# First score block and last weighing block over 128 columns instead of 256 in a hybrid encoder block on Trainium2

## The chip, the cores and the metric

The kernel runs on one core of one Trainium2 chip. The core has a matrix engine (TensorE, PE in the profile, with PEld for its weight loads), VectorE (DVE), ScalarE (ACT), GpSimd (POOL) and SyncE (SP, which issues the large loads). The metric is the time of one execution on the device in microseconds (us); several runs are given by their median.

## The reference

One layer over 512 positions and 1024 features, in float32. The part that matters here is the attention: 16 heads of 64 features over chunks of 64 positions, in which each position reads its own chunk and the 8 chunks before it. With 512 positions that is everything up to the end of its own chunk.

```python
def reference(x, ...):
    xn = rmsnorm(h, norm_mix_g[l])
    u = jnp.einsum('bsd,de->bse', xn, w_in[l])
    q, k, v, xr, gr, ga, gb = jnp.split(u, splits, axis=-1)
    ya = chunked_band_attention(q, k, v, rel_table[l]) @ w_attn_out[l]
    ...                                   # conv and RG-LRU branch: hr
    yb = (hr * jax.nn.gelu(gr)) @ w_rnn_out[l]
    ...                                   # g_a, g_b: gates
    h = h + (g_a * ya + g_b * yb) @ w_o[l]
    hn = rmsnorm(h, norm_ffn_g[l])
    g, up = jnp.split(hn @ w_ffn_in[l], 2, axis=-1)
    h = h + (jax.nn.silu(g) * up) @ w_ffn_out[l]
    return rmsnorm(h, final_norm_g)

def chunked_band_attention(q, k, v, rel_table):
    ...
    s = jnp.einsum('bnqhd,bnkhd->bhnqk', q, kb) * scale + bias     # own chunk and 8 before
    s = jnp.where(valid[None, None, :, None, :], s, NEG_INF)
    p = jax.nn.softmax(s, axis=-1)
    o = jnp.einsum('bhnqk,bnkhd->bnqhd', p, vb)
```

## The kernel before

**Precision.** A float32 operand is split into two parts of a reduced type, fp32r: hi is the rounded value, lo the rest (`split`, L78 to L81: a copy on ScalarE at L80, a subtraction on VectorE at L81). A projection (`mm3`, L72 to L76) is three matmuls: hi with hi, hi with lo, lo with hi. In the profile's rows these operands are printed as f32. Every matmul is preceded by its own weight load.

**Order of the work.** First come a norm, the recurrent branch and the gates, then the attention of 16 heads, then the output projections and a feed-forward part. A scheduler orders the instructions of each engine when the program is built; the source order is only its input. The attention's loop over heads calls `transposed`, `scores` of the next head, `weigh`, and between them `fill`, which puts in projections of q, k, v and a gate that are ready, so that TensorE has work while the softmax runs. These projections use 512 moving columns (v: 256).

**Scores** (`scores`, L611). The 512 queries are 4 blocks of 128 (`qb`). Block `qb` sees the keys of blocks 0 to `qb`, w = (qb + 1) x 128 columns. Two matmuls (L624 with the hi part of k, L625 with the lo part) write w columns into PSUM, for `qb` = 0 however 256, of which 128 are used. VectorE adds the bias and takes the row's maximum (L627), ScalarE takes the exponential and the sum (L628), VectorE the reciprocal (L629), GpSimd scales (L631).

**Transposes** (`transposed`, L634). The probabilities are transposed by TensorE in 10 pieces of 128 x 128 (L643) into three PSUM tiles: keys of block 0 (512 columns of queries), block 1 (384), and blocks 2 and 3 together (256 + 128). They are split into `pp` (L645, through L80 and L81). In the third tile `pp[2]` the columns 256 to 384 are filled with zeros by GpSimd (L637), and the columns of key block 3 are put behind them, at 384 to 512, by a split of their own.

**Weighing** (`weigh`, L652). For each key block, two matmuls (hi and lo of `pp`, L663) add values times probabilities into the last n query columns of one PSUM tile: n is 512, 384, 256 and, for the last key block, 256 again, where the first 128 of these columns are the zeros.

Of the kernel before, what the change touches and what calls it, by code (L numbers as in the profile page):

```python
# [36 lines left out]
def block_kernel(ctx: ExitStack, tc: tile.TileContext, x, norm_mix_g, w_in, b_merge, rel_table,  # L37
# [3 lines left out]
    pe, dve, act, pool, sp = nc.tensor, nc.vector, nc.scalar, nc.gpsimd, nc.sync  # L41
# [4 lines left out]
    def opened(name, bufs=1, side="left"):  # L46
        st = ExitStack()
        return st, st.enter_context(pool_of(name, bufs, side))
# [17 lines left out]
    def f(ap):  # L66
        return ap.bitcast(F32)

    def mm_tile(name, tag="mm"):
        return ps.tile([P, S], F32, tag=tag, bufs=4 if tag == "mm" else 2, name=name)  # L70
# [7 lines left out]
    def split(hi, lo, src):  # L78

        act.activation(hi, src, AF.Copy)  # L80
        dve.tensor_sub(lo, src, f(hi))  # L81
# [311 lines left out]
    def bias_tile(h):  # L393
        b = aw.tile([P, S], F32, tag="bias", bufs=2, name=f"bias{h}")
        src = ext_d[h:h + 1, 0:S]
        band = bass.AP(tensor=src.tensor, offset=src.offset, ap=[[1, P], [1, S]])
        sp.dma_start(out=b[:], in_=band)
        pool.memset(b[64:128, 448:512], NEG)
        return b
# [150 lines left out]
    def blocks(ap):  # L550
        return ap.rearrange("p (b i) -> p b i", i=P)

    def backwards(ap):
        return blocks(ap)[:, :, ::-1]

    def halves(e):
        own, other = slice(e * HD, e * HD + HD), slice(HD - e * HD, 2 * HD - e * HD)
        return own, other
# [52 lines left out]
    def scores(h):  # L611
        pr, e = divmod(h, 2)
        q, kh, kl = qk[pr]
        bias = bias_tile(h)
        lsum = cp.tile([P, NT], F32, tag="lsum", bufs=2, name=f"l{h}")
        nmax = cp.tile([P, NT], F32, tag="nmax", bufs=2, name=f"m{h}")
        rl = cp.tile([P, NT], F32, tag="rl", bufs=2, name=f"rl{h}")
        prob = [aw2.tile([P, (qb + 1) * P], F32, tag=f"p{qb}", name=f"p{h}_{qb}") for qb in range(NT)]
        for qb in range(NT):
            w = (qb + 1) * P  # L620
            wm = max(w, 256)
            sc = mm_tile(f"s{h}_{qb}") if qb == 2 else ps.tile([P, S], F32, tag="s", bufs=2, name=f"s{h}_{qb}")
            qs = q[:, e, qb * P:(qb + 1) * P]
            pe.matmul(sc[:, 0:wm], qs, kh[:, e, 0:wm], start=True, stop=False)  # L624
            pe.matmul(sc[:, 0:wm], qs, kl[:, e, 0:wm], start=False, stop=True)  # L625

            dve.tensor_tensor_reduce(prob[qb][:], sc[:, 0:w], bias[:, S - w:S], -1.0, 3e38, ALU.add, ALU.min, nmax[:, qb:qb + 1])  # L627
            act.activation(prob[qb][:], prob[qb][:], AF.Exp, bias=nmax[:, qb:qb + 1], scale=-1.0, accum_out=lsum[:, qb:qb + 1])  # L628
        dve.reciprocal(rl[:], lsum[:])  # L629
        for qb in range(NT):  # L630
            pool.tensor_scalar(prob[qb][:], prob[qb][:], rl[:, qb:qb + 1], 1.0, ALU.mult, ALU.mult)  # L631
        return prob

    def transposed(h, prob):  # L634

        pp = [aw2.tile([P, 2, S], F32R, tag="pt", bufs=4, name=f"pp{h}_{i}") for i in range(3)]
        pool.memset(f(pp[2][:, :, 256:384]), 0.0)  # L637
        for i, kbs in enumerate(((0,), (1,), (2, 3))):
            pt = ps.tile([P, S], F32, tag="t", bufs=2, name=f"pT{h}_{i}")
            for kb in kbs:  # L640
                for qb in range(kb, NT):
                    at = qb - min(kb, 2) if kb < 3 else 2
                    pe.transpose(pt[:, at * P:(at + 1) * P], prob[qb][:, kb * P:(kb + 1) * P], ident[:])  # L643
            for at, lo, n in (((0, 0, 512),), ((0, 0, 384),), ((0, 0, 256), (384, 256, 128)))[i]:
                split(pp[i][:, 0, at:at + n], pp[i][:, 1, at:at + n], pt[:, lo:lo + n])  # L645
        return pp

    aT = []
# [3 lines left out]
    def weigh(h, pp):  # L652
        pr, e = divmod(h, 2)
        own, other = halves(e)
        if e == 0:
            oacc.append(tg_.tile([P, S], F32, tag="tg", name=f"oacc{pr}"))
        acc = oacc[pr]
        po = mm_tile(f"o{h}")
        for kb in range(NT):
            i, lo, n = ((0, 0, 512), (1, 0, 384), (2, 0, 256), (2, 256, 256))[kb]  # L660
            st = vs[pr // 2][kb][:, pr % 2, 2 * e:2 * e + 2].rearrange("p a d -> p (a d)")
            for part in range(2):
                pe.matmul(po[:, S - n:S], st, pp[i][:, part, lo:lo + n], start=kb == 0 and part == 0, stop=kb == NT - 1 and part == 1)  # L663
        act.activation(acc[own, :], po[other, :], AF.Copy)
        dve.tensor_add(acc[own, :], po[own, :], acc[own, :])
        if e == 1:
            if pr % 2 == 0:
                aT_pairs.append(rnp.tile([P, 2, 2, S], F32R, tag="big", bufs=4, name=f"aT{pr}"))
            o = aT_pairs[-1][:, pr % 2]
            split(blocks(o[:, 0]), blocks(o[:, 1]), backwards(acc[:]))  # L670
            aT.append(o)
# [23 lines left out]
    for j in range(KT):  # L695
        if j == 6:
            prob = scores(0)
        po = mm_tile(f"po_yb{j}")
        project(po, weights(f"yb{j - j % 2}"), j % 2, rnn)
        dve.scalar_tensor_tensor(zB[j], zB[j], 1.0, po[:], ALU.add, ALU.mult)  # L700
    for h in range(HEADS):
        pp = transposed(h, prob)
        if h + 1 < HEADS:
            prob = scores(h + 1)
        fill(1.25 + 1.5 * h)
        weigh(h, pp)
        fill(2.0 + 1.5 * h)
# [115 lines left out]
    sc_stack, sc = opened("sc", 2)  # L823
# [100 lines left out]
    for i, ((t, at), po) in enumerate(zip(pieces, pos)):  # L924
        for k0, wf in zip(ks[late:], wfs):
            out_tile(t, po, k0, wf, at)
        n = 1 + i // 4
# [30 lines left out]
```

## Time and profile before

| | |
|---|---|
| median of 3 runs | 896.61 us (894.88 to 899.5) |
| profiled execution, time | 896.52 us |
| profiled execution, span | 894.7 us |
| granted TensorE clock | 0.995 |
| TensorE busy | 876.4 us, 5220 matmuls |
| VectorE, ScalarE, GpSimd busy | 554.3, 474.0, 133.4 us |
| score matmuls | 235 to 431 us after the span's start |
| weighing matmuls | 261 to 454 us |

The profile is of one execution. Busy time of TensorE counts each matmul's record from start to modelled end; neighbouring records overlap. A row of a group names the source line, the engine, the operation, output and inputs, the shape, the count, then busy time and mean length, then the idle time of the engine ahead of the group and what ended it.

### The profile page before, as it was taken

What the parts mean: (1) busy time and instruction counts of PE and PEld (TensorE: products, weight loads), DVE (VectorE), ACT (ScalarE), POOL (GpSimd) and SP (SyncE); (2) the same over time, 40 slices, a digit from 0 to 9 for tenths busy, and PEclk for the clock granted to TensorE, in tenths of its full rate; (3) what the DMA queues carried; (4) which work ended last, traced back from release to release, by engine and by line L of the source; (5) the groups of instructions that cost most, each with busy time, mean ns of one, the idle gap of its engine ahead of it and who ended that gap; (6) DMA issues with size and microseconds to landing.
All of it is one profiled execution on the core that took longest, in us unless ns stands there. A gap on an engine that the chain in (4) does not pass through costs nothing.

```text
span 894.7 us, 13342 instructions
## 1 busy us (share of the span) xinstructions
PE 876.4 (98%) x5220; PEld 779.1 (87%) x5220; DVE 554.3 (62%) x863; ACT 474.0 (53%) x841; POOL 133.4 (15%) x168
## 2 busy tenths in 40 slices
PE   8999999999999999999999999899999999999997
PEld 5988888888888889797888889899999999888886
DVE  6776556563466676566547455998788887463203
ACT  7566546642257666566533365556555556722203
POOL 4012112120013222232100002500000001300200
PEclk9999999999999999999999999999999999999999
DMA  7323223433332232232223521333433333253102
GB/s 263 95 72 117 85 83 93 119 95 95 106 106 72 84 105 61 75 105 68 68 69 126 210 76 43 95 119 98 139 95 95 96 106 107 95 189 121 43 1 95
DMA packets 85023, 89.05 MB, mean 100 GB/s; under 512 B 5344, under 2 KB 73552, under 8 KB 84960
## 3 DMA queue, kind: packets, MB, share of 16 engines
q1 hardware_dynamic: 83584, 84.73, 30.6%
q10 hardware_dynamic: 1376, 3.47, 1.0%
q8 instruction: 41, 0.67, 0.3%
q14 instruction: 22, 0.18, 0.1%
HBM read 86.05 MB, written 2.14 MB: 99 GB/s over the span
## 4 chain that ended last, share of the span: by engine, by line
PE 92%; DVE 3%; ACT 2%; DMA 1%; issue 1%; POOL 1%; SPq 0%; DVEq 0%; POOLq 0%; ACTq 0%
PE po_out L74 5%; PE po_out L76 4%; PE po_out L75 4%; PE p_fu L76 2%; PE p_fu L75 2%; PE p_fu L74 2%; PE p_fg L74 2%; PE p_fg L75 2%; PE p_fg L76 2%; PE o L663 2%; PE pT L643 2%; PE po_ga L74 2%; PE po_q L75 2%; PE po_q L74 2%; PE q_fg L76 2%; PE po_ga L75 2%
## 5 line engine op out<-in xcount | busy, mean ns | idle before, releaser
L75 PE MATMUL po_out<-whl_fo,act_hi 128*128 128x512 f32 (+1 forms) x198 | 72.4, 366 | 0.0
L74 PE MATMUL po_out<-whl_fo,act_hi 128*128 128x512 f32 (+1 forms) x198 | 72.4, 366 | 0.0
L76 PE MATMUL po_out<-whl_fo,act_lo 128*128 128x512 f32 (+1 forms) x198 | 71.6, 365 | 0.0
L81 DVE TENSOR_TENSOR whl_fo<-raw_fo,whl_fo 128x1024 fp32r<-128x1024 f32 x22 | 27.6, 1262 | 45.5 <-ACT whl_fo L80 45.1
L631 POOL TENSOR_SCALAR p<-p,rl 128x128 f32<-128x128 f32 (+1 forms) x64 | 37.6, 611 | 83.2 <-DVE rl L629 82.6
L80 ACT ACTIVATE whl_fo<-raw_fo 128x1024 fp32r<-128x1024 f32 x22 | 22.9, 1056 | 49.3 <-PE po_out L76 33.9
L628 ACT ACTIVATE p<-p,m 128x128 f32<-128x128 f32 (+3 forms) x64 | 35.5, 556 | 20.1 <-DVE m L627 19.8
L627 DVE CUSTOM_DVE_ANT_0 p<-s,bias 128x128 f32<-128x128 f32 (+3 forms) x64 | 29.8, 487 | 22.4 <-PE s L625 21.6
L76 PEld LDWEIGHTS po_out<-whl_fo,act_lo 128*128 128x128 f32 x198 | 37.3, 189 | 6.0
L75 PEld LDWEIGHTS po_out<-whl_fo,act_hi 128*128 128x128 f32 x198 | 37.4, 189 | 6.0
L74 PEld LDWEIGHTS po_out<-whl_fo,act_hi 128*128 128x128 f32 x198 | 37.4, 189 | 5.9
L663 PE MATMUL o<-pp,v 128*128 128x256 f32 (+2 forms) x128 | 35.3, 336 | 3.0 <-ACT pp L80 3.0
L843 POOL TENSOR_TENSOR act_lo<-act,act_hi 128x1024 fp32r<-128x1024 f32 x4 | 10.5, 2622 | 185.6 <-ACT act_hi L842 184.1
L75 PE MATMUL po_v<-whl_v,xnT 128*128 128x256 f32 x128 | 36.9, 288 | 0.0
L81 DVE TENSOR_TENSOR pp<-pT,pp 128x256 fp32r<-128x256 f32 (+2 forms) x64 | 30.4, 486 | 10.4 <-ACT pp L80 9.9
L74 PE MATMUL po_v<-whl_v,xnT 128*128 128x256 f32 x128 | 36.6, 286 | 0.0
L76 PE MATMUL po_v<-whl_v,xnT 128*128 128x256 f32 x128 | 36.4, 285 | 0.0
L80 ACT ACTIVATE pp<-pT 128x256 fp32r<-128x256 f32 (+2 forms) x64 | 26.6, 433 | 10.7 <-DVE pp L81 6.3
L75 PE MATMUL po_xr<-xnT,whl_xr 128*128 128x512 f32 (+1 forms) x80 | 27.9, 354 | 1.0 <-DVE xnT L331 1.0
L81 DVE TENSOR_TENSOR whl_fu_s<-s_fu,whl_fu_s 128x1024 fp32r<-128x1024 f32 x20 | 25.3, 1280 | 5.8 <-ACT whl_fu_s L80 5.7
L643 PE MATMUL pT<-ident,p 128*128 128x128 f32 x160 | 27.5, 273 | 0.8 <-POOL p L631 0.7
L663 PEld LDWEIGHTS o<-pp,v 128*128 128x128 f32 x128 | 22.8, 189 | 5.9 <-ACT pp L80 1.8
(354 smaller groups left out, 3096.0 us busy)
## 6 DMA issues: line engine op xcount, KB each, us to landing
raw_fg<-in_w_ffn_in_dram SPq DMA_DIRECT2D x22, 512.0 KB, 4.5
raw_fu<-in_w_ffn_in_dram SPq DMA_DIRECT2D x22, 512.0 KB, 3.5
raw_fo<-in_w_ffn_out_dram SPq DMA_DIRECT2D x22, 512.0 KB, 4.3
raw_qk<-in_w_in_dram SPq DMA_DIRECT2D x32, 256.0 KB, 3.2
raw_xr<-in_w_in_dram SPq DMA_DIRECT2D x8, 512.0 KB, 4.7
raw_gr<-in_w_in_dram SPq DMA_DIRECT2D x8, 512.0 KB, 3.4
raw_ga<-in_w_in_dram SPq DMA_DIRECT2D x8, 512.0 KB, 3.8
raw_gb<-in_w_in_dram SPq DMA_DIRECT2D x8, 512.0 KB, 3.5
```

The lines of the kernel that those rows point to most:

```text
L74: pe.matmul(o, sh, mh, start=start, stop=False, skip_group_check=parts)
L75: pe.matmul(o, sh, ml, start=False, stop=False, skip_group_check=parts)
L76: pe.matmul(o, sl, mh, start=False, stop=stop, skip_group_check=parts)
L80: act.activation(hi, src, AF.Copy)
L81: dve.tensor_sub(lo, src, f(hi))
L627: dve.tensor_tensor_reduce(prob[qb][:], sc[:, 0:w], bias[:, S - w:S], -1.0, 3e38, ALU.add, ALU.min, nmax[:, qb:qb + 1])
L628: act.activation(prob[qb][:], prob[qb][:], AF.Exp, bias=nmax[:, qb:qb + 1], scale=-1.0, accum_out=lsum[:, qb:qb + 1])
L631: pool.tensor_scalar(prob[qb][:], prob[qb][:], rl[:, qb:qb + 1], 1.0, ALU.mult, ALU.mult)
L643: pe.transpose(pt[:, at * P:(at + 1) * P], prob[qb][:, kb * P:(kb + 1) * P], ident[:])
L663: pe.matmul(po[:, S - n:S], st, pp[i][:, part, lo:lo + n], start=kb == 0 and part == 0, stop=kb == NT - 1 and part == 1)
L843: (pool if i in (0, 1, 2, 4) else dve).tensor_sub(lo[:], o[:], f(hi[:]))
```

## The change

The score matmuls of query block 0 take 128 columns instead of 256. The weighing matmuls of key block 3 take 128 columns instead of 256, so the zeros ahead of them are not needed: the memset goes, key block 3 is put right behind the first 256 columns, and the third transposed tile is split in one piece of 384 columns instead of 256 and 128. Lines behind the first edit move up by one and later by two in the changed source.

```diff
@@ scores
             w = (qb + 1) * P
-            wm = max(w, 256)
             ...
-            pe.matmul(sc[:, 0:wm], qs, kh[:, e, 0:wm], start=True, stop=False)
-            pe.matmul(sc[:, 0:wm], qs, kl[:, e, 0:wm], start=False, stop=True)
+            pe.matmul(sc[:, 0:w], qs, kh[:, e, 0:w], start=True, stop=False)
+            pe.matmul(sc[:, 0:w], qs, kl[:, e, 0:w], start=False, stop=True)
@@ transposed
-        pool.memset(f(pp[2][:, :, 256:384]), 0.0)
         ...
-            for at, lo, n in (((0, 0, 512),), ((0, 0, 384),), ((0, 0, 256), (384, 256, 128)))[i]:
-                split(pp[i][:, 0, at:at + n], pp[i][:, 1, at:at + n], pt[:, lo:lo + n])
+            n = (512, 384, 384)[i]
+            split(pp[i][:, 0, 0:n], pp[i][:, 1, 0:n], pt[:, 0:n])
@@ weigh
-            i, lo, n = ((0, 0, 512), (1, 0, 384), (2, 0, 256), (2, 256, 256))[kb]
+            i, lo, n = ((0, 0, 512), (1, 0, 384), (2, 0, 256), (2, 256, 128))[kb]
```

## The prediction

> **What bounds the kernel now.** I read the page first: the busy times and the chain that ended last.
>
> ```profile
> span 894.7 us, 13342 instructions
> PE 876.4 (98%) x5220; PEld 779.1 (87%) x5220; DVE 554.3 (62%) x863; ACT 474.0 (53%) x841; POOL 133.4 (15%) x168
> ...
> PE 92%; DVE 3%; ACT 2%; DMA 1%; issue 1%; POOL 1%; SPq 0%; DVEq 0%; POOLq 0%; ACTq 0%
> ```
>
> TensorE (PE) is busy nearly throughout and makes 92% of the chain. A busy PE is not yet a PE at its peak, because the records of neighbouring matmuls overlap. What counts is the pitch: the time from the start of one matmul to the start of the next. The table of stretches gives it where a stretch holds one shape. Its columns are the length, then busy time and count of PE, of the weight loads (PEld), of VectorE, ScalarE and GpSimd, then the granted clock, the DMA share and GB/s.
>
> ```profile
> 100.00:150.00 50.00, 50.00 (x222) 41.42 (x221) 30.29 (x34) 28.61 (x37) 9.06 (x7) 1.00 0.29 87
> ...
> 600.00:650.00 50.00, 50.00 (x419) 50.00 (x418) 42.08 (x59) 30.17 (x55) 0.00 (x0) 1.00 0.39 117
> ```
>
> The first stretch holds projections over 512 columns: 50/222 = 225.2 ns each. The second holds feed-forward blocks over 256 columns: 50/419 = 119.3 ns each, and there the weight loads fill all of the 50 us. Both run at the full granted clock (1.00). From 256 to 512 columns the pitch grows by 105.9 ns.
>
> The attention, where the change sits, is the third stretch:
>
> ```profile
> 260.00:435.00 175.00, 170.03 (x1004) 149.96 (x1003) 112.67 (x259) 114.28 (x261) 47.49 (x94) 0.99 0.28 82
> ```
>
> PE is idle there for 175.00 - 170.03 = 4.97 us. The table of waits names what ended that idle time (total us, times, longest):
>
> ```profile
> PE o L663 <- ACT pp L80: 3.0, 2, 1.5
> PE s L624 <- ACT kh L586: 1.2, 3, 0.8
> PE pT L643 <- POOL p L631: 0.7, 2, 0.3
> ```
>
> So the attention too is set by the matmul stream, not by the softmax or the copies. A matmul that gets cheaper or dearer moves the end by nearly its full difference; work taken off the other engines can return at most these 4.97 us.
>
> **The change, part by part.** First, the matmuls. For each of 16 heads the two score matmuls of the first query block (L624, L625) and the two weighing matmuls of the last key block (L663) go from 256 columns to 128. That is 16 x 4 = 64 matmuls. The number of matmuls and of weight loads stays, since each matmul loads its own weights. Grouped by shape, before (busy us, mean ns of one):
>
> ```profile
> L643 PE MATMUL pT<-ident,p 128*128 128x128 f32 x160 | 27.5, 273 | 0.8 <-POOL p L631 0.7
> ...
> L74 PE MATMUL po_gb<-xnT,whl_gb 128*128 128x512 f32 x64 | 24.9, 389 | 0.0
> ...
> L663 PE MATMUL o<-pp,v 128*128 128x256 f32 x64 | 16.6, 294 | 3.0 <-ACT pp L80 3.0
> ...
> L74 PE MATMUL p_fg<-hn,whl_fg_a 128*128 128x256 f32 x40 | 11.3, 283 | 0.0
> ...
> L624 PE MATMUL s<-kh,q 128*128 128x256 f32 x32 | 9.0, 315 | 1.2 <-ACT kh L586 1.2
> ...
> L625 PE MATMUL s<-kl,q 128*128 128x256 f32 x32 | 8.4, 293 | 0.0
> ```
>
> The trace has no product of reduced-precision operands (fp32r in the source, printed as f32) that is narrower than 256 columns. So its price must be bounded.
>
> From below: if the line through 512 and 256 columns went on, 128 columns would cost 119.3 - 105.9/2 = 66.3 ns. That is 53 ns less for each of 64, or -3.4 us.
>
> Between: the only 128-column rows are the transposes (L643). In the chain in order of time (start, us, what) runs of them stand by themselves:
>
> ```profile
> 438.57 0.33 PE pT L643 x3
> ...
> 440.18 0.44 PE pT L643 x4
> ```
>
> Each adds 0.11 us. So a 128-column instruction here costs 110 ns, nearly what a 256-column one costs. With that price the change saves 119.3 - 110 = 9.3 ns each, 0.6 us in all. The Trainium skill, page "TensorE: Matmul & The Clock Gate", section on LDWEIGHTS, puts a weight load at its columns divided by 1.2 ns, an estimated 107 ns for 128 columns; the 110 ns of this trace agree with a pitch held by the load, and by that figure the saving would be 64 x 12 ns = 0.8 us.
>
> From above: if a narrow fp32r product loses its one trip per column and the operands make four trips, it streams 4 x 128 = 512 column times, and the nearest row is the 512-column matmul: 225.2 ns. That is 105.9 ns more for each of 64, or +6.8 us. If each of the four trips also carried its own load, the price would be 4 x 110 = 440 ns, 64 x 321 ns = +20.5 us.
>
> I take the four trips at 225.2 ns. The reason is what the rows do and do not show. The single trip per column is measured from 256 columns up, and only there. The one 128-column row is of another kind: a transpose moves data through unchanged, and its record is 273 ns long where the line through 389 and 283 ns would give 283 - 53 = 230 ns. It doesn't show that a narrow product keeps its single trip, and it does show that the rate per column falls to about half (110/128 = 0.86 ns against 119.3/256 = 0.47 ns). Given a loss of rate, the ends are lopsided: at most 3.4 us can be won, and 6.8 us or more lost. This is a judgement, no reading: I give it six in ten. The Trainium skill, page "FP8 and Floating Point Precision", section TensorE Precision Notes, says that true FP32 takes four passes through the array and that a reduced form reads the same four bytes and truncates; no run here shows which of the two a narrow product gets.
>
> Second, the copies behind the transposes. The third transposed tile was split into hi and lo in two pieces, and is now split in one (mean ns after the bar):
>
> ```profile
> L80 ACT ACTIVATE pp<-pT 128x384 fp32r<-128x384 f32 x15 | 7.3, 486 | 0.1
> ...
> L80 ACT ACTIVATE pp<-pT 128x256 fp32r<-128x256 f32 x14 | 5.3, 379 | 2.1 <-PE pT L643 1.9
> ...
> L80 ACT ACTIVATE pp<-pT 128x128 fp32r<-128x128 f32 x14 | 3.8, 270 | 4.5 <-DVE pp L81 4.4
> ...
> L81 DVE TENSOR_TENSOR pp<-pT,pp 128x384 fp32r<-128x384 f32 x15 | 8.2, 549 | 0.0
> ...
> L81 DVE TENSOR_TENSOR pp<-pT,pp 128x256 fp32r<-128x256 f32 x14 | 5.9, 418 | 2.4 <-ACT pp L80 2.2
> ...
> L81 DVE TENSOR_TENSOR pp<-pT,pp 128x128 fp32r<-128x128 f32 x14 | 4.0, 287 | 1.9 <-ACT pp L80 1.8
> ```
>
> ScalarE saves 379 + 270 - 486 = 163 ns and VectorE 418 + 287 - 549 = 156 ns per head. That lies beside matmuls, except where PE waited for this tile, which it did twice (3.0 us). I take 2 x (163 + 156) = 0.6 us, rounded to -0.5 us; the ends are 0 and -3.0 us. A reverse cost is possible too: the first 256 columns could be copied after two of its three transposes, and now the copy waits for the third, 0.11 us per head, hidden like the rest.
>
> Third, the zero fill. GpSimd loses 16 memsets:
>
> ```profile
> L637 POOL MEMSET pp<- 128x256 f32 x15 | 4.7, 316 | 47.2 <-PE o L663 30.0 <-PE pT L643 14.9 <-PE s L625 2.0
> ```
>
> Its queue waited 47.2 us there for a free tile, with the next scaling (L631) and copy (L587) behind it. PE hardly waits for these: 0.7 us for L631 above. I take nothing, with -0.7 us as the end.
>
> Fourth, the order. The program's PE order is the same up to the first head's weighing and then differs in places, because the scheduler places each instruction anew. I take nothing; the bound is that the 4.97 us of idle vanish or double, 5 us to either side.
>
> The sum: the profiled execution took 896.5 us, 1.8 us beside its span, and stands 0.1 us under the median of 896.6. With +6.8 - 0.5 = +6.3 us it becomes 902.8 us.
>
> **The rivals.** The weight load sets the pitch: a narrow product keeps its single trip and costs the transposes' 110 ns. Then -0.6 - 0.5 us gives 895.4 us, no change, and decides if a 128-column product costs under about 199 ns (64 x 79.7 ns less 0.5 us reach the 4.6 us that lie between 896.5 us and the edge of slower, 901.1 us). For it speaks the 110 ns row, and that the loads already fill the whole stretch at 256 columns. Against it: the row is a transpose. Two trips of 128 columns, 256 column times, end within 0.6 us of it. I give it 0.25.
>
> The price follows the line: 66.3 ns, -3.4 - 0.5 us, 892.6 us, 0.4% less. The 110 ns row speaks against it, because these matmuls load weights too. I give it 0.04, and 0.04 more to the same with an order that wins idle time, below 892.1 us.
>
> Four trips, each with its load: +20.5 - 0.5 us, 916.5 us. Nothing in the rows speaks for it but the load's pace: 0.07.
>
> **How the numbers follow.** Forecast 0.60, rivals 0.25, 0.08 and 0.07. A measurement of this kernel can tell about 0.5%, 4.5 us, from no change, so "same" is 892.1 to 901.1 us. The forecast lies 1.7 us above that edge; with the uncertain order I leave a tenth of it below, 0.06. Slower: 0.54 + 0.07 = 0.61. Same: 0.25 + 0.06 + 0.04 = 0.35. Faster: 0.04. The range must hold the forecast and the first rival: from 894.5 us to 907 us (the forecast and most of a doubled idle time); the forecast's own range is 899 to 907 us.
>
> **What would show it.** In the changed kernel's groups by shape, the 128-column rows of the score and weighing lines: means near 389 ns, as 512 columns have, and starts 225 ns apart where they follow one another, prove four trips. Means of 230 to 273 ns with starts 110 ns apart prove the load; 66 ns apart, the line. PE busy in the attention should grow by 6 us and its idle time stay near 5 us. The copies should show 16 rows fewer on both engines with a 384-column form x32, and no memset of pp. I am wrong if the 128-column records are not longer than the 256-column ones, or if the time moves while they are, through idle PE that these rows don't explain.

## The result and the profile after

The changed kernel takes 899.56 us (median of 8 runs, 898.08 to 902.32) against 896.4 us before (median of 8, 894.88 to 899.5). The ratio is 1.0038, 95% interval [1.0024, 1.0053]: 0.4% slower, clear of noise but inside the 0.5% that the prediction called "same". The page of the changed kernel begins:

```profile
span 897.8 us, 13305 instructions
...
PE 876.4 (98%) x5220; PEld 777.0 (87%) x5220; DVE 552.0 (61%) x847; ACT 472.0 (53%) x825; POOL 130.9 (15%) x152
```

TensorE is busy for 876.4 us, as before, and the span is 3.1 us longer. So the idle time grew: 897.8 - 876.4 = 21.4 us, where it was 894.7 - 876.4 = 18.3 us. The delay arises in the attention. The first score matmul starts at 235.5 us in both kernels, within 0.1 us, and the first product of `q_fg` in the feed-forward part at 566.02 us before and at 569.12 us after. The table of stretches and the table of waits show most of the added idle time there:

```profile
260.00:435.00 175.00, 167.53 (x984) 146.73 (x983) 107.66 (x239) 110.02 (x238) 45.60 (x78) 0.99 0.28 80
```

```profile
PE pT L641 <- POOL p L630: 5.3, 5, 1.6
...
PE s L623 <- ACT kh L586: 0.9, 1, 0.9
...
PE o L661 <- ACT pp L80: 0.5, 2, 0.3
```

The idle time there is 7.47 us where it was 4.97 us, 2.5 us more. The weighing waits less for its copies (0.5 us, before 3.0), but the transposes wait 5.3 us (before 0.7) for the scaled probabilities, which GpSimd makes. The groups by shape show the narrow products:

```profile
L641 PE MATMUL pT<-ident,p 128*128 128x128 f32 x160 | 29.6, 277 | 6.1 <-POOL p L630 5.3
...
L661 PE MATMUL o<-pp,v 128*128 128x256 f32 x32 | 8.1, 280 | 0.0
...
L661 PE MATMUL o<-pp,v 128*128 128x128 f32 x32 | 5.4, 249 | 0.0
...
L624 PE MATMUL s<-kl,q 128*128 128x128 f32 x16 | 4.2, 262 | 0.0
L623 PE MATMUL s<-kh,q 128*128 128x128 f32 x16 | 4.2, 259 | 0.9 <-ACT kh L586 0.9
```

A product over 128 columns is recorded at 249 to 262 ns, shorter than one over 256 columns (280 ns), and far from the 389 ns of 512 columns. The narrow products are not where the time went.

The order in time shows what did. These are the last score matmul of a head (L624), its softmax on VectorE and ScalarE, the scaling on GpSimd (L630), and the transposes of the same head (L641). The columns are start and length in us, engine, line, operation, shapes and count, and in brackets the idle time before:

```profile
362.83 0.40 PE L624 MATMUL s<-kl,q 128*128 128x512 f32 x1
...
363.37 0.69 DVE L626 CUSTOM_DVE_ANT_0 p<-s,bias 128x512 f32<-128x512 f32 x1
...
364.11 0.73 ACT L627 ACTIVATE p<-p,m 128x512 f32<-128x512 f32 x1
...
364.32 1.38 PE L661 MATMUL o<-pp,v 128*128 128x512 f32 x8
...
364.95 0.18 DVE L628 RECIPROCAL rl<-l 128x4 f32<-128x4 f32 x1 [0.22 <-ACT p L627]
...
365.33 3.02 POOL L630 TENSOR_SCALAR p<-p,rl 128x128 f32<-128x128 f32 x4 [18.39 <-DVE rl L628]
...
365.75 1.45 PE L641 MATMUL pT<-ident,p 128*128 128x128 f32 x5
...
366.38 1.40 DVE L81 TENSOR_TENSOR whl_v<-raw_v,whl_v 128x1024 fp32r<-128x1024 f32 x1 [0.27 <-ACT whl_v L80]
...
368.40 0.44 PE L641 MATMUL pT<-ident,p 128*128 128x128 f32 x2 [1.19 <-POOL p L630]
```

TensorE comes to the transposes 2.9 us after the last scores (362.83 to 365.75), when GpSimd has just begun. Five transposes then take 2.65 us where they need 0.55 us at 0.11 us each: 2.1 us lost, of which the overlapping records hide a part. The same picture stands near 313 and 417 us.

The scaling itself is also slow here. Its fourth piece, over 512 columns, starts at 366.69 us and takes 1.66 us. In the 16 heads of this trace that piece takes 0.69 to 0.70 us 13 times and 1.65 to 1.66 us three times, in just these three heads, each time beside a split of 1024 columns on VectorE (L81, 1.40 us in the lines above). So of the 2.1 us about 1 us goes with the slower piece, by an estimate from these lengths; that the split on VectorE slows GpSimd is not shown, since no run moves one without the other. One more long wait, 1.56 us at 282 us, has a slow piece of the scaling too (256 columns, 2.55 us where the median is 0.48), but 6.7 us between the last scores and the transposes. It comes with the old order too (1.1 us, in the first experiment below), so it is not the layout's.

In the kernel before, the head in this place has its last score matmul at 359.09 us and its first transpose at 369.64 us:

```profile
359.09 0.39 PE L625 MATMUL s<-kl,q 128*128 128x512 f32 x1
...
369.64 0.27 PE L643 MATMUL pT<-ident,p 128*128 128x128 f32 x1
```

So the scheduler has laid the instructions of TensorE out anew, and in three heads this layout leaves too little work between the scores and the transposes: 15 matmuls, where the kernel before has at least 30 in every head.

### The profile page after: what moved, and what is told of

The parts are those of the page before. It is cut to its first block, busy times and chain, and to the rows that moved or that the text cites. A ratio compares the mean times of both kernels' runs of the same rounds, so it can differ in the third digit from the quotient of the medians.

```text
span 897.8 us, 13305 instructions
## 1 busy us (share of the span) xinstructions
PE 876.4 (98%) x5220; PEld 777.0 (87%) x5220; DVE 552.0 (61%) x847; ACT 472.0 (53%) x825; POOL 130.9 (15%) x152
## 5 line engine op out<-in xcount | busy, mean ns | idle before, releaser
L630 POOL TENSOR_SCALAR p<-p,rl 128x128 f32<-128x128 f32 (+1 forms) x64 | 37.9, 610 | 162.7 <-DVE rl L628 157.0
L81 DVE TENSOR_TENSOR whl_fo<-raw_fo,whl_fo 128x1024 fp32r<-128x1024 f32 x22 | 27.6, 1261 | 45.4 <-ACT whl_fo L80 44.7
L641 PE MATMUL pT<-ident,p 128*128 128x128 f32 x160 | 29.6, 277 | 6.1 <-POOL p L630 5.3
L81 DVE TENSOR_TENSOR pp<-pT,pp 128x384 fp32r<-128x384 f32 (+1 forms) x48 | 27.9, 596 | 8.0 <-ACT pp L80 7.7
L80 ACT ACTIVATE pp<-pT 128x384 fp32r<-128x384 f32 (+1 forms) x48 | 24.1, 523 | 16.3 <-PE pT L641 16.1
L641 PEld LDWEIGHTS pT<-ident,p 128*128 128x128 f32 x160 | 19.4, 140 | 11.2 <-POOL p L630 8.7
L81 DVE TENSOR_TENSOR whl_fu_s<-s_fu,whl_fu_s 128x1024 fp32r<-128x1024 f32 x20 | 25.3, 1279 | 5.8 <-ACT whl_fu_s L80 5.7
L661 PE MATMUL o<-pp,v 128*128 128x512 f32 (+3 forms) x128 | 27.8, 321 | 0.5 <-ACT pp L80 0.5
```

## The experiments

**The first four: order or price.** Three theories were put against each other. Order: a narrow product costs the weight load's pace, and the loss comes from the place of the transposes. Price: each narrow product costs some 50 ns more than the records show. Copy: the one split in place of two comes late. In the first two kernels the instructions keep their widths but take the other kernel's order of TensorE in the attention, by edges between neighbouring TensorE instructions that fix who comes first and add no wait:

```diff
+    mms = [i for i in nc.cur_bb.bb.instructions if i.engine == mybir.EngineType.PE and type(i).__name__ == "InstMatmult"]
+    seq = [mms[at + k] for at, n in PE_ORDER for k in range(n)]
+    for later, earlier in zip(seq[1:], seq):
+        tc.add_manual_dep(later, earlier.name, mybir.DependencyInfo(mybir.DependencyClass.NoSync, mybir.DependencyReason.DATA), reason="order")
```

*New widths, old order* (the changed kernel with the list taken from before):

> The changed kernel with TensorE's order in the attention held to that of before (order edges only, no waits). Order theory (a 128-column product costs the weight load's pace, about 10 ns less than a 256-column one, and the 3 us come from transposes that the new order puts ahead of their inputs): 895.8 us, within 0.1% of before or below it, idle time of TensorE in the attention back to about 5 us. Price theory (each of the 64 narrow products costs about 50 ns more, hidden in the records): 899.6 us as the changed kernel. Copy theory (the one split in place of two comes late): 899.6 us too, with waits of the weighing matmuls for pp.

Measured: 897.55 us against 895.98 us, ratio 1.0017 [1.0006, 1.0027].

```profile
PE s L623 <- ACT kh L586: 3.0, 3, 1.8
...
PE o L661 <- ACT pp L80: 1.6, 1, 1.6
PE pT L641 <- POOL p L630: 1.5, 2, 1.1
```

The transposes' waits fall from 5.3 to 1.5 us and more than half of the loss is gone, with narrow products throughout. It isn't all gone, and the 895.8 us that were expected were missed: the copies and the softmax on the other engines were ordered anew around the fixed list, the scores now wait 3.0 us for the keys (before 1.2), and the granted clock was lower in most of these runs (last section). The price theory alone would have left 899.6 us.

*Old widths, new order* (the kernel before with the list taken from the changed one):

> The kernel before (256 columns, zero fill, two splits) with TensorE's order in the attention held to that of the changed kernel. Order theory: 900.2 us, with about 5 us of waiting of the transposes for the scaling on GpSimd. Price theory and copy theory: 896.4 us as before.

Measured: 899.94 us, ratio 1.0042 [1.0027, 1.0057]: the whole loss, without one narrow product and with both splits. The waits show at the weighing rather than at the transposes, against the expectation:

```profile
PE o L663 <- POOL p L631: 3.4, 3, 1.1
PE o L663 <- DVE pp L81: 2.8, 3, 0.9
```

*Only the scores narrow* and *only the weighing narrow* each do half of the change:

```diff
-            wm = max(w, 256)          # scores only: nothing else is edited
+            wm = w
```

```diff
+            wm = max(w, 256)          # weighing only: added to the changed kernel
-            pe.matmul(sc[:, 0:w], qs, kh[:, e, 0:w], start=True, stop=False)
-            pe.matmul(sc[:, 0:w], qs, kl[:, e, 0:w], start=False, stop=True)
+            pe.matmul(sc[:, 0:wm], qs, kh[:, e, 0:wm], start=True, stop=False)
+            pe.matmul(sc[:, 0:wm], qs, kl[:, e, 0:wm], start=False, stop=True)
```

> Only the scores of the first query block over 128 columns; the weighing keeps 256, zero fill and two splits. The order of TensorE stays near that of before (274 places of 5220 differ). Order theory: 896.0 us, between 895 and 897. Price theory: half of the loss, 898.0 us. Copy theory: 896.4 us.

> Only the weighing over 128 columns, without zero fill and with one split; the scores keep 256 columns. The order of TensorE is that of the changed kernel but for 3 places. Order theory: 899.9 us, the whole loss, with the same waits of the transposes for the scaling. Price theory: half of it, 898.0 us. Copy theory: 899.6 us.

Measured: scores only 895.29 us, ratio 0.9994 [0.9983, 1.0004]; weighing only 899.84 us, ratio 1.0046 [1.0027, 1.0064]. Both have 32 narrow products; one loses nothing and the other everything. The second one has the changed kernel's order and its waits:

```profile
PE pT L642 <- POOL p L631: 5.3, 5, 1.5
```

**Take the wait away.** If the place of the last scores is the cause, then moving these alone should bring the time back. In the changed kernel's own order, the two matmuls over 512 columns of the last query block move ten places ahead, in the three heads near 308, 358 and 407 us (the list is fixed as above, rearranged so):

```diff
+for s in (1563, 1859, 2155):      # places of the first of the two in TensorE's order
+    order[s - 10:s + 2] = order[s:s + 2] + order[s - 10:s]
```

> The changed kernel with its own order of TensorE, but for three heads the two score matmuls of the last query block stand ten projection matmuls (2.2 us) earlier, so that their softmax and scaling are done before the transposes come. Order theory: the waits of the transposes for the scaling near 313, 366 and 417 us (some 1.5 us each) go, 4 to 4.5 us less than the changed kernel, 895.3 us. If the narrow products or the single split had their own price in the 3 us: 898 us or more, though the waits go.

Measured: 894.69 us against 896.03 us before, ratio 0.9984 [0.9971, 0.9997]. Divided by the changed kernel's 1.0038 this is 0.9946, 4.8 us less. It is also the fastest version here, 0.2% under the kernel before. The gain is not the clock's: at a mean granted clock of 0.997 these are 893.8 us (3 runs) against 898.1 us (1 run) of the changed kernel. Its waits, and the same stretch in the order of time on TensorE and on GpSimd:

```profile
PE s L623 <- ACT kh L586: 3.0, 4, 0.9
...
PE pT L641 <- POOL p L630: 1.6, 1, 1.6
```

```profile
357.71 0.39 PE L624 MATMUL s<-kl,q 128*128 128x512 f32 x1
...
362.69 1.05 PE L641 MATMUL pT<-ident,p 128*128 128x128 f32 x7
```

```profile
361.20 2.05 POOL L630 TENSOR_SCALAR p<-p,rl 128x128 f32<-128x128 f32 x4 [17.37 <-DVE rl L628]
```

Now 5.0 us lie between the scores and the transposes, the scaling starts 1.5 us ahead of these, and the seven run without a wait. The scaling takes 2.05 us for its four pieces, not 3.02: it ends at 363.25 us, as the split on VectorE begins (363.24 us). So the move took away both the short distance and the slow piece, and this run does not part the two. What is left of the transposes' waits, 1.6 us in one piece, is the one at 282 us, which was not touched.

**Two other orders.** The changed kernel with the order of the scores-only kernel, by a list as above:

> The changed kernel with TensorE's order in the attention held to that of the kernel with narrow scores only. Order theory: 895.0 us, 0.3 us under that kernel for 32 more narrow products, if the other engines follow; up to 897.5 us where their new order brings waits of its own, which then show as idle time of TensorE. Price theory: 897 us and more without such idle time.

Measured: 895.32 us, ratio 0.9995 [0.9984, 1.0005]. All 64 narrow products at no loss.

The changed kernel with the third tile's split in two, again without zero fill, in the order that the scheduler then finds:

```diff
-            n = (512, 384, 384)[i]
-            split(pp[i][:, 0, 0:n], pp[i][:, 1, 0:n], pt[:, 0:n])
+            for at, n in (((0, 512),), ((0, 384),), ((0, 256), (256, 128)))[i]:
+                split(pp[i][:, 0, at:at + n], pp[i][:, 1, at:at + n], pt[:, at:at + n])
```

> The changed kernel, but the third transposed tile split in two pieces as before (256 and 128 columns), still without zero fill. The scheduler then makes a third order, which differs from that of before in 502 places and from that of the changed kernel in 743. Order theory: the long waits of the transposes for the scaling near 313, 366 and 417 us are gone, 896 us, between 895 and 897.5. Price theory: 899.6 us as the changed kernel. Copy theory: 896.4 us.

Measured: 898.28 us, ratio 1.0017 [1.0004, 1.0029]. The waits of the transposes are gone, as expected, but the size missed, for the weighing waits in their place:

```profile
PE o L661 <- ACT pp L80: 4.4, 3, 1.5
```

So a third order brings a third set of waits. Undoing the merged split alone leads to another order, so the split matters for the order; but that order is not the one of before either, so it is not the split alone. Why the scheduler chose as it did is not shown.

**The price by itself.** Into the kernel before, ahead of the attention, 192 products of fp32r operands whose sum nobody reads:

```diff
+    with tc.high_priority():
+        for n in (512, 384, 256, 192, 128, 64):
+            probe = ps.tile([P, S], F32, tag="s", bufs=2, name=f"probe{n}")
+            for i in range(32):
+                pe.matmul(probe[:, 0:n], xnT[i % KT][:, i // KT % 2, 0:P], xnT[(i + 3) % KT][:, 0, 0:n], start=i == 0, stop=i == 31)
```

> The kernel before with 192 more matmuls ahead of the attention, 32 each over 512, 384, 256, 192, 128 and 64 moving columns of fp32r, each with its own weights, whose sum nobody reads; only the pitch counts. Weight-load theory: 225, 172, 119, 110, 110, 110 ns, floor at the load. Four trips below 256: 225, 172, 119, 330, 225, 119 ns. The line: 225, 172, 119, 93, 66, 40 ns.

The stretches from the start of each group of 32 to the start of the next, for these instructions alone (length, TensorE and weight loads busy, clock, DMA share, GB/s; the counts take in neighbours that reach into a stretch):

```profile
174.83:182.08 7.25, 7.25 (x32) 6.01 (x32) 1.00 0.16 55
182.08:187.65 5.57, 5.57 (x33) 5.57 (x32) 1.00 0.00 0
187.65:191.48 3.83, 3.83 (x34) 3.83 (x33) 1.00 0.00 0
191.48:195.03 3.55, 3.55 (x34) 3.55 (x33) 1.00 0.00 0
195.03:198.58 3.55, 3.55 (x35) 3.55 (x33) 1.00 0.03 5
```

Divided by 32: 226.6 ns for 512 columns, 174.1 for 384, 119.7 for 256, 110.9 for 192 and 110.9 for 128. From 256 columns up the pitch follows the columns; below it stands at 111 ns. Of the sixth group, 64 columns, the first 21 start at full clock, from 198.58 to 200.89 us: 110 ns each, the same floor. The rest fell into a stretch of half clock.

That the weight loads are busy all the time does not yet prove that they set the floor, for they are so at 384 and 256 columns too, where the columns count. The stream of the attention says more. Here are the last three weighing products of one head and the projections behind them, in the changed kernel and, in the same order of TensorE, with old widths. The first of the three has 256 columns in both; the other two have 128 in the changed kernel:

```profile
302.74 0.45 PE L661 MATMUL o<-pp,v 128*128 128x256 f32 x3
303.03 0.45 PE L76 MATMUL po_q<-xnT,whl_qk 128*128 128x512 f32 x1
303.31 0.39 PE L74 MATMUL po_q<-xnT,whl_qk 128*128 128x512 f32 x1
303.54 0.40 PE L75 MATMUL po_q<-xnT,whl_qk 128*128 128x512 f32 x1
```

```profile
301.51 0.52 PE L663 MATMUL o<-pp,v 128*128 128x256 f32 x3
301.86 0.40 PE L76 MATMUL po_q<-xnT,whl_qk 128*128 128x512 f32 x1
302.09 0.40 PE L74 MATMUL po_q<-xnT,whl_qk 128*128 128x512 f32 x1
302.33 0.39 PE L75 MATMUL po_q<-xnT,whl_qk 128*128 128x512 f32 x1
```

The three take 0.29 us instead of 0.35, but the projection behind them takes 0.28 us instead of 0.23. At the last start shown, 0.80 against 0.82 us, the two narrow products have won 0.02 us together. In the 16 heads the second narrow product starts 56 to 63 ns after the first, so a narrow product itself can be that short; most of what it wins is paid back by its successor. Over the places that have neither idle time nor half clock, 50 narrow products win 0.58 us together, 11.5 ns each, near the 8.8 ns of the pitch measurement. The floor of 111 ns is therefore not the narrow product's own length, but the pace of something that can run ahead of it, as the weight load does. No run varies the load itself, so that it is the load remains argued.

## Why the prediction was right, and where it was not

The direction was right, the time (899.56 us) lies in the range of 894.5 to 907 us, and in that of the forecast by itself (899 to 907 us). The outcome that was held most likely, slower than 901.1 us (0.61), did not come; "same" (0.35) did, with +3.2 us where +6.3 us were forecast. The mechanism was wrong, and that the time still fell into the forecast's own range is luck: the price was forecast at +6.8 us and the order at nothing, while the runs show -0.6 us for the price and +3.8 us for the order (the old widths in the new order, 0.42%).

- **What bounds the kernel**: right. TensorE's stream sets the end, and what delays it in the attention, 3.1 us, is found again in the span. That work taken off the other engines can return at most the 4.97 us of idle time leaves out the clock: the attention before has one stretch of half clock, 3.4 us long (last section).
- **The price of a narrow product**: the step that failed. Four trips at 225.2 ns were forecast, +6.8 us; measured are 110.9 ns, 64 x (119.7 - 110.9) = -0.6 us. The first rival, the 110 ns of the transposes' rows, has it within a nanosecond and was given 0.25. The transposes were the nearest row, and setting them aside as another kind of instruction was the error: both load 128 columns of weights for 128 moving columns, and both came out at 110 to 111 ns.
- **The sign for the line**: starts 66 ns apart were to prove the line, and in the place of the change the second narrow product does start 56 to 63 ns after the first. Yet the line is wrong, because the product behind the pair starts late. The spacing of two neighbours is no price; it is read over a stretch that takes in what stands behind them.
- **The weight load and the four passes**: the Trainium skill's page "TensorE: Matmul & The Clock Gate", section on LDWEIGHTS, gives a load as its columns divided by 1.2 ns, an estimated 107 ns for 128 columns. The floor of 110.9 ns agrees with it. The four passes of true FP32, on the Trainium skill's page "FP8 and Floating Point Precision", section TensorE Precision Notes, do not show in these products: 128 and 192 columns take the same 110.9 ns.
- **The copies**: right in kind. The rows are 16 fewer on each of both engines, and the 384-column form stands there 32 times at the length that was taken, 486 ns:

```profile
L80 ACT ACTIVATE pp<-pT 128x384 fp32r<-128x384 f32 x32 | 15.5, 486 | 8.8 <-PE pT L641 8.6
```

  The weighing's waits for them fell by 2.5 us, inside the ends of 0 and -3.0 us; -0.5 us was taken. How much of this is the copies' own is not shown: with the merged split and the old order 1.6 us of these waits are left.
- **The order**: taken at nothing, with a bound of 5 us to either side. This is the term that decided, +3.8 us. The transposes' waits, held to be worth 0.7 us at most, grew to 5.3 us. The bound took it in; the forecast did not.
- **What would prove it wrong** did: the 128-column records are not longer than those of 256 columns, and the time moved through waits of TensorE that these rows don't explain.

## What to carry to other kernels

Below the width at which the pitch stops following the columns, fewer columns buy almost nothing: here 128 columns cost 111 ns and 256 cost 120 ns in a steady stream. Where a scheduler orders the program, a small edit buys a new order too, and that can outweigh the edit: read the distance between a producer's last matmul and the matmul that needs its result, before and after. To tell order from price, hold one order over both programs, and undo one half of the edit at a time.

## What the runs showed of the hardware beyond that

A wait of 1.5 us on TensorE can be followed by a stretch of half clock, and then costs more than itself. In the kernel before, such a wait ends at 362.8 us, and the granted clock is half for the next 3.4 us, with half as many matmuls as in the 3.4 us after:

```profile
363.40:366.80 3.40, 3.40 (x10) 2.82 (x11) 0.90 (x3) 1.05 (x2) 1.96 (x5) 0.50 0.66 191
366.80:370.20 3.40, 3.40 (x20) 2.92 (x19) 0.48 (x3) 0.59 (x2) 1.18 (x3) 1.00 0.00 1
```

By these counts the stretch costs about 1.7 us, half of its length. Not every wait of this length is followed by one (of four waits of 1.2 to 1.6 us in the attention of the changed kernel, one, at 316.5 us), and it differs from run to run. Among 25 runs of the kernel before, the 6 with a mean granted clock of 0.997 took 894.9 us on average, the 14 with 0.995 took 896.1 us, and the 2 with 0.993 took 898.0 us. The loss of the change is not the clock's: at 0.995 the changed kernel took 898.9 us (3 runs). The new widths in the old order took 896.2 us at 0.995 (4 runs) and 897.6 us at 0.993 (6 runs), within 0.1 us of the kernel before at the same clock or under it. So the 0.17% that the order theory left over go with the lower clock of most of these runs; the profiled one has two stretches of half clock in the attention, the kernel before has one. What makes the clock fall is not shown. It also fell while TensorE never stood still: in the measurement of the price it was half from 200.9 us on, 2.3 us into the group of 64 columns:

```profile
198.58:200.90 2.32, 2.32 (x24) 2.32 (x23) 1.00 0.00 0
200.90:203.00 2.10, 2.10 (x13) 2.10 (x12) 0.51 0.00 0
```
